# The two kinds of unit in a feed-forward block change places, and five edits go with it

## The chip, the cores and the metric

The kernel runs on one core of one Trainium2 chip. The metric is the device time of one execution in microseconds, as the median of several runs. Five engines of the core work at once, each through a queue of its own in program order: TensorE (PE in the profile; PEld is its weight load), VectorE (DVE), ScalarE (ACT), GpSimd (POOL) and SyncE (SP), which here issues nearly all DMAs. Matrix products are written to PSUM; everything else lies in SBUF.

## The reference

Two layers of an encoder on 512 tokens with 1024 features in float32. Each layer is a half-step feed-forward block, a mixer (attention with twelve heads of 64 in three dilations, and a pooling branch), and a second half-step feed-forward block:

```python
def swiglu(h, w_gate, w_up, w_down):
    return (jax.nn.silu(h @ w_gate) * (h @ w_up)) @ w_down

for l in range(DEPTH):
    x = x + 0.5 * swiglu(rmsnorm(x, ffn1_norm[l]), ffn1_w_gate[l], ffn1_w_up[l], ffn1_w_down[l])
    ...  # mixer: x = x + concat(pooling, attention) @ w_out[l]
    x = x + 0.5 * swiglu(rmsnorm(x, ffn2_norm[l]), ffn2_w_gate[l], ffn2_w_up[l], ffn2_w_down[l])
return rmsnorm(x, final_norm)
```

`rmsnorm` divides by the root of the mean square over the features and multiplies by a gain. The hidden width is 2816.

## The kernel before, in words

x lies transposed in eight tiles of 128 features by 512 tokens, called chunks here. Each float32 operand of a matmul is split into a rounded high part and a low part (the remainder), and a product is three matmuls: high by high, low by high, high by low. For a weight tile ScalarE makes the high part (`whi`, line 357) and VectorE the remainder (`wlo`, line 360).

The hidden width of a feed-forward block is cut into five units of 512 features and one small unit of 256. `UNITS` gives their order; before, the small one (number `NU`) comes first. The gate and up products of a unit are done by Strassen's scheme: seven block products in the order `PORD = (1, 2, 6, 5, 7, 3, 4)` instead of eight. Five of them need sums. On the side of x, `Norm.fold` makes them: for each of the last four chunks ScalarE makes a scaled copy and a high part, and VectorE makes the remainder (`al`, line 446), four sums of 256 columns (`s_n`, lines 447 to 450) and two remainders of these (`sl`, lines 457 and 458). On the side of the weights `total` (lines 254 and 258) makes a pair of sums for product 6, `across` one for product 7 and `every` one for product 4, all on VectorE. Products 1 and 2 need no sums: product 1 works with the first four chunks, product 2 with the last four.

A product of a big unit comes in two steps (cp 0 and 1), each with a weight tile of its own and half of the chunks: 12 matmuls of 512 columns. A product of the small unit is one step with one weight tile: 24 matmuls of 256 columns. `take` gives out weights: it splits two tiles ahead of the one that is taken (`AHEAD`), and makes the sums of a product three places ahead. In each product `px` or `pz` are a pair of PSUM banks; the pools of tags A to D have two banks each. The down matmuls of a unit (`pd_f`, two output chunks per weight tile) stand between the product steps of the next one, at the steps in `DOWN_AT`; each ends in a residual on VectorE (line 708, in the mixer line 937).

The next block's norm works while x is finished: `chunk(c)` folds chunk c and squares it (`square`, on ScalarE), and VectorE adds the squares up (line 480). After the third product (in the mixer, after the first values) `finish_col` sums them over the features with a few matmuls (`ms_n`, line 495), and GpSimd takes the power -0.5.

What runs when on VectorE is decided by three lists: work put into `later` is issued at the next `flush`, `lazy` at the one behind it, `slow` after two. The tables for the rotary embedding are a generator of seven pieces; in the first block a piece is issued after each step from the seventh on in the second unit, and on into the third if some are left.

Of the kernel before, what the change touches and what calls it, by code (L numbers as in the profile page):

```python
# [34 lines left out]
            1.0313385246263351e-05]  # L35
GW = S + 3 * P
NU = 5
UNITS = (NU, 0, 1, 2, 3, 4)
PORD = (1, 2, 6, 5, 7, 3, 4)
DOWN_AT = ((5, 7, 9, 11), (5, 9))  # L40
TWO_PI = 2.0 * math.pi
C1 = 6.28125
C2 = float(np.float32(np.int32(round((TWO_PI - C1) * 2.0**21)) / 2.0**21))
# [35 lines left out]
def trunk(ctx: ExitStack, tc: tile.TileContext, a: dict):  # L79
# [39 lines left out]
    def startup(norm):  # L119
        nc.sync.dma_start(x[0], a["xT"][0])  # L120
        load(2)
        nc.gpsimd.dma_start(vecs, a["vecs"])
        nc.vector.memset(ones, 1.0 / D)
        nc.vector.memset(npow, -0.5)
        idle = const.tile([P, S], mybir.dt.bfloat16, name="idle")
        nc.vector.memset(idle, 0.0)
        nc.scalar.activation(npow, npow, AF.Copy)
        for c in range(1, 4):
            nc.sync.dma_start(x[c], a["xT"][c])
        load()  # L130
        for c in range(4, KD):
            nc.sync.dma_start(x[c], a["xT"][c])
        pump()
        nc.sync.dma_start(ident, a["ident"])
        pos = a["positions"]
        nc.gpsimd.dma_start(col, a["col"])
        nc.gpsimd.dma_start(pos_i, bass.AP(tensor=pos.tensor, offset=pos.offset, ap=[[0, P], [1, S]]))
        warm = bank("D", "warm")
        for _ in range(WARM):
            nc.tensor.matmul(warm, idle[:, 0:P], idle, start=True, stop=True)  # L140
        for c in range(KD):
            norm.fold(c)
            if c < 2:
                divide(c)
            if c == 4:
                divide()
            flush()

# [61 lines left out]
    class Job:  # L210


        def __init__(self, key, n, needs, get, pre=None, done=None):
            self.key, self.n, self.needs, self.get, self.pre, self.done = key, n, needs, get, pre, done
            self.part = None

    jobs, loads = [], []
    AHEAD, SLOTS = 2, 11
    state = {"live": 0, "temps": 0, "load": 0, "split": 0, "taken": 0, "cap": SLOTS}

    def free():
# [7 lines left out]
    def product_jobs(i, l, u):  # L229

        small = u == NU
        cps = 1 if small else 2
        made, out = {}, []

        def quarter(kh, n, cp):
            ap = a[f"gs{i}"][l, kh, n] if small else a[f"gu{i}"][l, u, kh, n, cp]
            made[kh, n, cp] = Load(ap, D)

        quarters = [(0, 0), (1, 0)]
        for kh, n in quarters:  # L240
            for cp in range(cps):
                quarter(kh, n, cp)
        for cp in range(cps):
            quarter(0, 1, cp)
            quarter(1, 1, cp)
        first = next(iter(made.values()))
        first.temps = cps
        loads.extend(made.values())
        both = {}

        def total(cp):

            b11, b12, b22 = (made[q + (cp,)].tile for q in ((0, 0), (0, 1), (1, 1)))
            nc.vector.tensor_tensor(b11, b11, b12, op=ALU.add)
            both[cp] = t4([P, D], F32, f"sum_{i}{l}_{u}_{cp}")
            state["live"] += 1
            state["temps"] -= 1
            nc.vector.tensor_tensor(both[cp], b11, b22, op=ALU.add)

        def across(cp):  # L260
            b12, b22 = made[0, 1, cp].tile, made[1, 1, cp].tile
            nc.vector.tensor_tensor(b12, b12, b22, op=ALU.add)

        def every(cp):
            b21 = made[1, 0, cp].tile
            nc.vector.tensor_tensor(b21, b21, both[cp], op=ALU.add)
            free()

        for p in PORD:
            for cp in range(cps):  # L270
                q = {k: made[k + (cp,)] for k in quarters + [(0, 1), (1, 1)]}
                key = ("g", i, l, u, p, cp)
                tile_of = lambda k, q=q: (lambda: q[k].tile)
                if p == 1:
                    job = Job(key, D, [q[0, 0]], tile_of((0, 0)))
                elif p == 2:
                    job = Job(key, D, [q[1, 0]], tile_of((1, 0)))
                elif p == 6:
                    job = Job(key, D, [q[0, 0], q[0, 1], q[1, 1]], lambda cp=cp: both[cp],
                              pre=lambda cp=cp: total(cp), done=lambda cp=cp: every(cp))  # L280
                elif p == 5:
                    job = Job(key, D, [], tile_of((0, 0)), done=free)
                elif p == 7:
                    job = Job(key, D, [], tile_of((0, 1)), pre=lambda cp=cp: across(cp), done=free)
                elif p == 3:
                    job = Job(key, D, [], tile_of((1, 1)), done=free)
                else:
                    job = Job(key, D, [], tile_of((1, 0)), done=free)
                out.append(job)
        return out  # L290
# [10 lines left out]
    def ffn_jobs(i, l):  # L301
        for n, u in enumerate(UNITS):
            pj = product_jobs(i, l, u)
            dj = down_jobs(i, l, UNITS[n - 1]) if n else []
            for z, job in enumerate(pj):
                jobs.append(job)
                if n and z in DOWN_AT[n == len(UNITS) - 1]:
                    jobs.append(dj.pop(0))
            jobs.extend(dj)
        jobs.extend(down_jobs(i, l, UNITS[-1]))  # L310

# [35 lines left out]
    def divide(half=None):  # L347
# [10 lines left out]

        def rest():
            nc.vector.tensor_tensor(lo[:, o:e], raw[:, o:e], hi[:, o:e].bitcast(F32), op=ALU.subtract)  # L360
            if half != 0 and job.done is not None:
                job.done()
        later.append(rest)
        if half != 0:
            state["split"] += 1
# [1 line left out]
    def take(*key):  # L367
# [2 lines left out]
        state["taken"] += 1  # L370
        while state["split"] < min(i + AHEAD + 1, len(jobs)):
            divide()
        nxt = i + AHEAD + 1
        if nxt < len(jobs) and jobs[nxt].pre is not None and all(ld.tile is not None for ld in jobs[nxt].needs):
            prepare_sums(jobs[nxt])
        pump()
        w, jobs[i].part = jobs[i].part, None
        return w
# [30 lines left out]
    class Norm:  # L409
# [62 lines left out]
        def square(self, c):  # L472
# [111 lines left out]
    def ffn(which, l, norm, nxt, first=False):  # L584
# [20 lines left out]
        def products(n, u):  # L605
            N = S if u < NU else S // 2
            w, cps = N // 2, 2 if u < NU else 1
            xs = [bank("AB"[n % 2], f"px_{nm}_{u}_{i}") for i in range(2)]
            zs = {}
            c = {}  # L610

# [30 lines left out]
            def step(p, cp):  # L642
                flush()
                hi, lo = take("g", which, l, u, p, cp)
                if p == 2 and cp == 0 or p == 5 and cp == 0:
                    zs.clear()
                    zs.update({i: bank("BA"[n % 2], f"pz{p}_{nm}_{u}_{i}") for i in range(2)})
                out = zs if p in (2, 5, 3) else xs
                ks = range(2 * cp, 2 * cp + 2) if cps == 2 else range(4)
                for i in range(2):  # L650
# [22 lines left out]
            for p in PORD:  # L673
                for cp in range(cps):
                    step(p, cp)
                    if turns and z >= 1:
                        for _ in range(2):
                            if turns:
                                turns.pop(0)()
                    if n and z in DOWN_AT[last]:  # L680
                        flush()
                        down(UNITS[n - 1], todo.pop(0))
                    if first and n in (1, 2) and z >= 6:
                        next(rotary, None)
                    z += 1
            tiles = w // P
# [407 lines left out]
```

## Time and profile before

| | |
|---|---|
| runs, us | 1920.46, 1922.04, 1922.73; median 1922.04 |
| profiled execution, us | 1919.58 |
| its span (first to last instruction), us | 1917.8 |
| mean granted clock of TensorE | 0.986 |
| busy, us: TensorE, VectorE, ScalarE, GpSimd | 1857.2 (97%), 1444.4 (75%), 950.4 (50%), 116.9 (6%) |

The profile comes from one execution. Busy time is the time in which an engine had an instruction in work; the granted clock is given as a share of the full 2.4 GHz, so that 0.5 is the lower level of 1.2 GHz. In a timeline each row has the start in us, the duration, the engine, the line of the kernel, the operation, the tile written and those read, the form, and in brackets how long the engine had been idle and what released it. Consecutive VectorE instructions overlap by some 0.08 us, so that the difference of two starts, not the duration, says how long one holds the queue.

The first feed-forward block runs from the start to about 385 us, the first mixer up to 617, the second block of layer 0 up to 969; layer 1 follows in the same way.

### The profile page before, as it was taken

What the parts mean: (1) busy time and instruction counts of PE and PEld (TensorE: products, weight loads), DVE (VectorE), ACT (ScalarE), POOL (GpSimd) and SP (SyncE); (2) the same over time, 40 slices, a digit from 0 to 9 for tenths busy, and PEclk for the clock granted to TensorE, in tenths of its full rate; (3) what the DMA queues carried; (4) which work ended last, traced back from release to release, by engine and by line L of the source; (5) the groups of instructions that cost most, each with busy time, mean ns of one, the idle gap of its engine ahead of it and who ended that gap; (6) DMA issues with size and microseconds to landing.
All of it is one profiled execution on the core that took longest, in us unless ns stands there. A gap on an engine that the chain in (4) does not pass through costs nothing.

```text
span 1917.8 us, 23563 instructions
## 1 busy us (share of the span) xinstructions
PE 1857.2 (97%) x8966; PEld 1551.3 (81%) x8966; DVE 1444.4 (75%) x2041; ACT 950.4 (50%) x1474; POOL 116.9 (6%) x105
## 2 busy tenths in 40 slices
PE   6989999999999999999989999999999989999998
PEld 5868888898877888888878888888888778888887
DVE  6996677647887986778688777675688688777675
ACT  6444344436665553444464444444476565444444
POOL 0000000013230000000000000000323200000000
PEclk7999999999999999999999999999999999999999
DMA  5223333125451233422313322340454223232321
GB/s 183 88 79 100 128 110 107 64 76 145 113 158 56 66 121 99 132 96 97 105 50 116 121 88 88 99 148 17 126 134 126 89 94 116 99 99 96 102 77 45
DMA packets 59696, 194.36 MB, mean 101 GB/s; under 512 B 7920, under 2 KB 8064, under 8 KB 59584
## 3 DMA queue, kind: packets, MB, share of 16 engines
q1 hardware_dynamic: 59440, 192.57, 31.9%
q8 instruction: 70, 1.15, 0.2%
q0 software_dynamic: 144, 0.29, 0.1%
q14 instruction: 42, 0.34, 0.1%
HBM read 171.87 MB, written 2.10 MB: 91 GB/s over the span
## 4 chain that ended last, share of the span: by engine, by line
PE 86%; DVE 8%; ACT 2%; issue 2%; DMA 1%; POOL 1%; SPq 0%; DVEq 0%; POOLq 0%; ACTq 0%
PE pd_f L384 8%; PE pd_f L383 8%; PE pd_f L382 8%; PE px_f L658 8%; PE px_f L655 8%; PE px_f L657 8%; PE pz_f L655 6%; PE pz_f L658 6%; PE pz_f L657 6%; PE pv_m L747 3%; PE ps_m L814 2%; PE pt_m L827 2%; PE pt_f L600 2%; DVE wlo L360 1%; PE po_m L843 1%
## 5 line engine op out<-in xcount | busy, mean ns | idle before, releaser
L360 DVE TENSOR_TENSOR wlo<-raw,whi 128x1024 fp32r<-128x1024 f32 (+2 forms) x421 | 502.0, 1198 | 55.4 <-ACT whi L357 50.4
L357 ACT ACTIVATE whi<-raw 128x1024 fp32r<-128x1024 f32 (+2 forms) x421 | 421.7, 1026 | 220.3 <-DVE wlo L360 63.9
L384 PE MATMUL pd_f<-ah_f,wlo 128*128 128x512 f32 (+1 forms) x736 | 282.2, 383 | 3.1 <-DVE wlo L360 3.1
L382 PE MATMUL pd_f<-ah_f,whi 128*128 128x512 f32 (+1 forms) x736 | 281.5, 382 | 1.0 <-ACT ah_f L400 1.0
L383 PE MATMUL pd_f<-al_f,whi 128*128 128x512 f32 (+1 forms) x736 | 280.7, 381 | 1.0 <-DVE al_f L403 1.0
L708 DVE SCALAR_TENSOR_TENSOR x<-pd_f,x 128x512 f32<-128x512 f32 x184 | 127.0, 690 | 168.8 <-PE pd_f L384 165.5
L592 ACT ACTIVATE c_f<-c_f,rcol_n 128x256 f32<-128x256 f32 (+1 forms) x144 | 70.3, 492 | 272.4 <-DVE c_f L637 102.5
L384 PEld LDWEIGHTS pd_f<-ah_f,wlo 128*128 128x128 f32 x736 | 138.7, 188 | 33.5 <-DVE wlo L360 7.7
L383 PEld LDWEIGHTS pd_f<-al_f,whi 128*128 128x128 f32 x736 | 138.8, 189 | 28.8 <-DVE al_f L403 2.3
L655 PE MATMUL px_f<-whi,ah_n 128*128 128x512 f32 (+1 forms) x384 | 145.9, 380 | 15.7 <-DVE x L937 11.5
L382 PEld LDWEIGHTS pd_f<-ah_f,whi 128*128 128x128 f32 x736 | 138.9, 189 | 27.4 <-ACT ah_f L400 1.9
L655 PE MATMUL px_f<-whi,sh_n 128*128 128x512 f32 (+1 forms) x384 | 144.1, 375 | 5.7 <-ACT c_f L622 5.7
L658 PE MATMUL px_f<-wlo,ah_n 128*128 128x512 f32 (+1 forms) x384 | 145.2, 378 | 1.2 <-DVE wlo L360 1.2
L658 PE MATMUL px_f<-wlo,sh_n 128*128 128x512 f32 (+1 forms) x384 | 144.1, 375 | 1.9 <-DVE wlo L360 1.9
L658 PE MATMUL pz_f<-wlo,sh_n 128*128 128x512 f32 (+1 forms) x384 | 143.3, 373 | 2.1 <-DVE wlo L360 2.1
L657 PE MATMUL px_f<-whi,al_n 128*128 128x512 f32 (+1 forms) x384 | 145.3, 378 | 0.0
L655 PE MATMUL pz_f<-whi,sh_n 128*128 128x512 f32 (+1 forms) x384 | 143.7, 374 | 0.6 <-DVE c_f L624 0.3
L657 PE MATMUL px_f<-whi,sl_n 128*128 128x512 f32 (+1 forms) x384 | 143.7, 374 | 0.0
L657 PE MATMUL pz_f<-whi,sl_n 128*128 128x512 f32 (+1 forms) x384 | 143.1, 373 | 0.0
L819 ACT ACTIVATE e_m<-e_m,nmx_m 128x512 f32<-128x512 f32 x96 | 69.4, 723 | 78.7 <-DVE nmx_m L817 78.1
L655 PEld LDWEIGHTS px_f<-whi,ah_n 128*128 128x128 f32 x384 | 74.3, 193 | 30.1 <-DVE x L937 11.9
L817 DVE CUSTOM_DVE_ANT_0 e_m<-ps_m,gbias 128x512 f32<-128x512 f32 x96 | 65.9, 686 | 33.8 <-PE ps_m L814 33.3
(206 smaller groups left out, 3580.4 us busy)
## 6 DMA issues: line engine op xcount, KB each, us to landing
raw<-in_gu SPq DMA_DIRECT2D x160, 512.0 KB, 3.3
raw<-in_dn SPq DMA_DIRECT2D x80, 512.0 KB, 3.3
raw<-in_wqk SPq DMA_DIRECT2D x24, 512.0 KB, 5.4
qq_m<-hl_q_m SPq DMA_DIRECT2D x48, 256.0 KB, 4.2
raw<-in_wo SPq DMA_DIRECT2D x16, 512.0 KB, 5.3
raw<-in_gs SPq DMA_DIRECT2D x15, 512.0 KB, 4.9
raw<-in_wv SPq DMA_DIRECT2D x16, 384.0 KB, 3.1
kk_m<-hl_k_m SPq DMA_DIRECT2D x48, 128.0 KB, 2.3
```

The source lines that it names most:

```text
L357: nc.scalar.activation(hi[:, o:e], raw[:, o:e], AF.Copy)
L360: nc.vector.tensor_tensor(lo[:, o:e], raw[:, o:e], hi[:, o:e].bitcast(F32), op=ALU.subtract)
L382: nc.tensor.matmul(ps, hi[:, o:o + P], act[0], start=start, stop=False)
L383: nc.tensor.matmul(ps, hi[:, o:o + P], act[1], start=False, stop=False)
L384: nc.tensor.matmul(ps, lo[:, o:o + P], act[0], start=False, stop=stop)
L592: nc.scalar.activation(c[:, :w], src[:, :w], AF.Silu, scale=r)
L655: nc.tensor.matmul(ps, bh, hi[:, o], start=(k == 0 and p in (1, 2, 5)), stop=False, skip_group_check=True)
L657: nc.tensor.matmul(ps, bl, hi[:, o], start=False, stop=False, skip_group_check=True)
L658: nc.tensor.matmul(ps, bh, lo[:, o], start=False, stop=(k == 3), skip_group_check=True)
L708: nc.vector.scalar_tensor_tensor(x[d], ps, 0.5, x[d], op0=ALU.mult, op1=ALU.add)
L817: nc.vector.tensor_tensor_reduce(e, ps, gbias[:, o:o + S], -0.125, 3.0e38, ALU.add, ALU.min, nmx[hd][:, it:it + 1])
L819: nc.scalar.activation(e, e, AF.Exp, bias=nmx[hd][:, it:it + 1], scale=-1.0, accum_out=den[hd][:, it:it + 1])
```

## The change

The unit order becomes one big unit, the small one, then the other four; `DOWN_AT` now has a row for each place in this order. Squares are added on GpSimd. `take` looks at five more jobs instead of one and makes the sums of any whose weights are being loaded and whose sources have been split. A piece of the rotary tables is issued at every fourth step from the third unit on. The PSUM tags A and B of the product banks change places. In the start-up two more weight tiles are loaded between the last pieces of x, and one more is split early. The core of the diff:

```diff
-UNITS = (NU, 0, 1, 2, 3, 4)
+UNITS = (0, NU, 1, 2, 3, 4)
-DOWN_AT = ((5, 7, 9, 11), (5, 9))
+DOWN_AT = ((), (3, 4, 5, 6)) + 3 * ((5, 7, 9, 11),) + ((5, 9),)
...
         for c in range(4, KD):
             nc.sync.dma_start(x[c], a["xT"][c])
+            if c in (5, 7):
+                load()
...
-            if c == 4:
+            if c in (3, 6):
                 divide()
...
-    AHEAD, SLOTS = 2, 11
+    AHEAD, EARLY, SLOTS = 2, 5, 11
...
-        nxt = i + AHEAD + 1
-        if nxt < len(jobs) and jobs[nxt].pre is not None and all(ld.tile is not None for ld in jobs[nxt].needs):
-            prepare_sums(jobs[nxt])
+        for job in jobs[i + AHEAD + 1:i + AHEAD + 1 + EARLY]:
+            if job.pre is not None and job.after.split and all(ld.tile is not None for ld in job.needs):
+                prepare_sums(job)
...
-                lazy.append(lambda: nc.vector.tensor_tensor(acc, acc, sq, op=ALU.add))
+                lazy.append(lambda: nc.gpsimd.tensor_tensor(acc, acc, sq, op=ALU.add))
...
-            xs = [bank("AB"[n % 2], f"px_{nm}_{u}_{i}") for i in range(2)]
+            xs = [bank("BA"[n % 2], f"px_{nm}_{u}_{i}") for i in range(2)]
-                    zs.update({i: bank("BA"[n % 2], f"pz{p}_{nm}_{u}_{i}") for i in range(2)})
+                    zs.update({i: bank("AB"[n % 2], f"pz{p}_{nm}_{u}_{i}") for i in range(2)})
...
-                    if n and z in DOWN_AT[last]:
+                    if z in DOWN_AT[n]:
-                    if first and n in (1, 2) and z >= 6:
+                    if first and n >= 2 and z % 4 == 3:
                         next(rotary, None)
```

How the instructions move is shown at two places. The first is VectorE's queue where layer 0's mixer ends and its second feed-forward block begins, right behind the residual of the last chunk (`x_71`), up to the remainder of the third weight tile. The names are tiles, with a number for each allocation. Before, the rows are:

```order
L480 TENSOR_TENSOR sq_n_0_5140<-sq_n_0_5140,sq_n_6_5291 128x512
L457 TENSOR_TENSOR sl_n_6_5290<-s_n_6_5288,sh_n_6_5289 128x512
L458 TENSOR_TENSOR sl_n_6_5290<-s_n_6_5287,sh_n_6_5289 128x512
L446 TENSOR_TENSOR al_n_3_5175<-xs_n_7_5336,ah_n_3_5174 128x512
L447 TENSOR_TENSOR s_n_7_5339<-xs_n_3_5172,xs_n_7_5336 128x256
L448 TENSOR_TENSOR s_n_7_5340<-s_n_7_5339,xs_n_3_5172 128x256
L449 TENSOR_TENSOR s_n_7_5339<-xs_n_3_5172 128x256
L450 TENSOR_TENSOR s_n_7_5340<-xs_n_7_5336,s_n_7_5340 128x256
L480 TENSOR_TENSOR sq_n_0_5140<-sq_n_0_5140,sq_n_7_5343 128x512
L457 TENSOR_TENSOR sl_n_7_5342<-s_n_7_5340,sh_n_7_5341 128x512
L458 TENSOR_TENSOR sl_n_7_5342<-s_n_7_5339,sh_n_7_5341 128x512
L360 TENSOR_TENSOR wlo_5358<-sum_5_0_5297,whi_5357 128x1024
```

In the changed kernel, right behind the same residual:

```order
L465 TENSOR_TENSOR sl_n_6_5292<-s_n_6_5290,sh_n_6_5291 128x512
L466 TENSOR_TENSOR sl_n_6_5292<-s_n_6_5289,sh_n_6_5291 128x512
L454 TENSOR_TENSOR al_n_3_5175<-xs_n_7_5338,ah_n_3_5174 128x512
L455 TENSOR_TENSOR s_n_7_5341<-xs_n_3_5172,xs_n_7_5338 128x256
L456 TENSOR_TENSOR s_n_7_5342<-s_n_7_5341,xs_n_3_5172 128x256
L457 TENSOR_TENSOR s_n_7_5341<-xs_n_3_5172 128x256
L458 TENSOR_TENSOR s_n_7_5342<-xs_n_7_5338,s_n_7_5342 128x256
L465 TENSOR_TENSOR sl_n_7_5344<-s_n_7_5342,sh_n_7_5343 128x512
L466 TENSOR_TENSOR sl_n_7_5344<-s_n_7_5341,sh_n_7_5343 128x512
L366 TENSOR_TENSOR wlo_5360<-raw_5104,whi_5359 128x1024
L256 TENSOR_TENSOR raw_5102<-raw_5102,raw_5362 128x1024
L260 TENSOR_TENSOR sum_0_1_5385<-raw_5102,raw_5364 128x1024
```

The squares (`sq_n`) are gone from the queue, the third remainder belongs to product 2 of the big unit (`raw_5104`) instead of product 6 of the small one, and the pair of sums for the second half of product 6 (`sum_0_1`) follows it.

The second place is VectorE at the start of layer 1, from the fold of the last chunk on. Before:

```order
L446 TENSOR_TENSOR al_n_3_8007<-xs_n_7_8135,ah_n_3_8006 128x512
L447 TENSOR_TENSOR s_n_7_8138<-xs_n_3_8004,xs_n_7_8135 128x256
L448 TENSOR_TENSOR s_n_7_8139<-s_n_7_8138,xs_n_3_8004 128x256
L449 TENSOR_TENSOR s_n_7_8138<-xs_n_3_8004 128x256
L450 TENSOR_TENSOR s_n_7_8139<-xs_n_7_8135,s_n_7_8139 128x256
L457 TENSOR_TENSOR sl_n_6_8111<-s_n_6_8109,sh_n_6_8110 128x512
L458 TENSOR_TENSOR sl_n_6_8111<-s_n_6_8108,sh_n_6_8110 128x512
L480 TENSOR_TENSOR sq_n_0_7936<-sq_n_0_7936,sq_n_7_8142 128x512
L457 TENSOR_TENSOR sl_n_7_8141<-s_n_7_8139,sh_n_7_8140 128x512
L458 TENSOR_TENSOR sl_n_7_8141<-s_n_7_8138,sh_n_7_8140 128x512
L360 TENSOR_TENSOR wlo_8160<-sum_5_0_8083,whi_8159 128x1024
L266 TENSOR_TENSOR raw_7730<-raw_7730,sum_5_0_8083 128x1024
```

In the changed kernel:

```order
L454 TENSOR_TENSOR al_n_3_8009<-xs_n_7_8135,ah_n_3_8008 128x512
L455 TENSOR_TENSOR s_n_7_8138<-xs_n_3_8006,xs_n_7_8135 128x256
L456 TENSOR_TENSOR s_n_7_8139<-s_n_7_8138,xs_n_3_8006 128x256
L457 TENSOR_TENSOR s_n_7_8138<-xs_n_3_8006 128x256
L458 TENSOR_TENSOR s_n_7_8139<-xs_n_7_8135,s_n_7_8139 128x256
L465 TENSOR_TENSOR sl_n_6_8111<-s_n_6_8109,sh_n_6_8110 128x512
L466 TENSOR_TENSOR sl_n_6_8111<-s_n_6_8108,sh_n_6_8110 128x512
L256 TENSOR_TENSOR raw_7746<-raw_7746,raw_7916 128x1024
L260 TENSOR_TENSOR sum_0_1_8163<-raw_7746,raw_7966 128x1024
L465 TENSOR_TENSOR sl_n_7_8141<-s_n_7_8139,sh_n_7_8140 128x512
L466 TENSOR_TENSOR sl_n_7_8141<-s_n_7_8138,sh_n_7_8140 128x512
L366 TENSOR_TENSOR wlo_8160<-raw_7768,whi_8159 128x1024
```

Here the second pair of sums (`sum_0_1`) stands ahead of the third remainder.

## Rows read from the trace of the kernel before

**Rows 1.** windows by stretch: span us, then busy us (instructions) by engine, clock, DMA

```profile
7.00:55.00 48.00, 33.37 (x176) 30.13 (x177) 38.24 (x66) 31.30 (x54) 1.03 (x1) 0.72 0.45 164
92.00:135.00 43.00, 36.37 (x153) 27.78 (x153) 42.05 (x59) 20.00 (x30) 0.00 (x0) 0.96 0.27 86
135.00:360.00 225.00, 225.00 (x1021) 186.34 (x1020) 162.63 (x188) 98.80 (x131) 0.00 (x0) 1.00 0.34 111
617.00:647.00 30.00, 23.73 (x177) 23.02 (x176) 26.05 (x43) 17.22 (x30) 1.02 (x1) 0.89 0.25 82
968.00:999.00 31.00, 22.97 (x164) 21.56 (x163) 27.53 (x46) 16.55 (x29) 1.01 (x1) 0.89 0.25 77
```

**Rows 2.** timeline of PE behind the first mixer: start, us, what [idle before]

```profile
616.88 0.39 PE L384 MATMUL po_m<-yhh_m,wlo 128*128 128x512 f32 x1
617.11 0.28 PE L655 MATMUL px_f<-whi,ah_n 128*128 128x256 f32 x1
617.22 0.28 PE L657 MATMUL px_f<-whi,al_n 128*128 128x256 f32 x1
...
624.47 0.58 PE L655 MATMUL px_f<-whi,ah_n 128*128 128x256 f32 x1 [5.76 <-DVE x L937]
...
634.53 0.95 PE L495 MATMUL ms_n<-ones,sq_n 128*128 128x1 f32 x8
```

**Rows 3.** timeline of PE in the stretch of the rotary tables

```profile
103.73 0.63 PE L382 MATMUL pd_f<-ah_f,whi 128*128 128x512 f32 x1
104.16 0.63 PE L383 MATMUL pd_f<-al_f,whi 128*128 128x512 f32 x1
```

**Rows 4.** timeline of DVE behind the first mixer

```profile
620.52 0.69 DVE L446 TENSOR_TENSOR al_n<-xs_n,ah_n 128x512 fp32r<-128x512 f32 x1
621.13 0.42 DVE L447 TENSOR_TENSOR s_n<-xs_n,xs_n 128x256 f32<-128x256 f32 x1
...
622.59 1.22 DVE L360 TENSOR_TENSOR wlo<-raw,whi 128x1024 fp32r<-128x1024 f32 x1
623.73 0.68 DVE L937 TENSOR_TENSOR x<-po_m,x 128x512 f32<-128x512 f32 x1
624.33 0.68 DVE L480 TENSOR_TENSOR sq_n<-sq_n,sq_n 128x512 f32<-128x512 f32 x1
...
630.51 1.23 DVE L360 TENSOR_TENSOR wlo<-sum,whi 128x1024 fp32r<-128x1024 f32 x1 [0.18 <-ACT whi L357]
```

**Rows 5.** groups by line and form: busy us, mean ns | idle before

```profile
L480 DVE TENSOR_TENSOR sq_n<-sq_n,sq_n 128x512 f32<-128x512 f32 x42 | 28.8, 685 | 0.6
```

**Rows 6.** timeline of DVE at the end of the attention, layer 0

```profile
557.21 1.70 DVE L403 TENSOR_TENSOR yh_m<-y_m,yh_m 128x512 fp32r<-128x512 f32 x1
558.83 2.32 DVE L360 TENSOR_TENSOR wlo<-raw,whi 128x1024 fp32r<-128x1024 f32 x1
561.07 0.68 DVE L403 TENSOR_TENSOR pl_m<-pt_m,ph_m 128x512 fp32r<-128x512 f32 x1
```

**Rows 7.** timeline of POOL in the same stretch

```profile
558.43 1.64 POOL L908 TENSOR_TENSOR m_pool_m<-r_pool_m,ic_pool_m 64x512 f32<-64x512 f32 x1
560.14 2.14 POOL L909 TENSOR_TENSOR m_pool_m<-m_pool_m,v_pool_m 128x512 f32<-128x512 f32 x1
```

**Rows 8.** timeline of DVE at the start of layer 1

```profile
963.60 0.69 DVE L708 SCALAR_TENSOR_TENSOR x<-pd_f,x 128x512 f32<-128x512 f32 x1 [0.29 <-PE pd_f L384]
...
984.43 1.22 DVE L360 TENSOR_TENSOR wlo<-sum,whi 128x1024 fp32r<-128x1024 f32 x1
```

**Rows 9.** timeline of PE at the start of layer 1

```profile
968.84 0.28 PE L655 MATMUL px_f<-whi,ah_n 128*128 128x256 f32 x1
...
988.43 0.95 PE L495 MATMUL ms_n<-ones,sq_n 128*128 128x1 f32 x8
```

**Rows 10.** timeline of DVE in the start-up

```profile
14.03 0.69 DVE L446 TENSOR_TENSOR al_n<-xs_n,ah_n 128x512 fp32r<-128x512 f32 x1 [0.94 <-ACT ah_n L439]
```

**Rows 11.** timeline of PE in the start-up

```profile
41.00 1.28 PE L495 MATMUL ms_n<-ones,sq_n 128*128 128x1 f32 x8 [2.55 <-DVE sq_n L480]
```

More of the change, by code (lines that the diff above doesn't have):

```diff
@@ L214, in __init__ @@
             self.key, self.n, self.needs, self.get, self.pre, self.done = key, n, needs, get, pre, done
-            self.part = None
+            self.part, self.after, self.split = None, None, False
     jobs, loads = [], []
-    AHEAD, SLOTS = 2, 11
+    AHEAD, EARLY, SLOTS = 2, 5, 11
     state = {"live": 0, "temps": 0, "load": 0, "split": 0, "taken": 0, "cap": SLOTS}
@@ L232, in product_jobs @@
         cps = 1 if small else 2
-        made, out = {}, []
+        made, out, firsts = {}, [], {}
         def quarter(kh, n, cp):
@@ L275, in product_jobs @@
                     job = Job(key, D, [q[0, 0]], tile_of((0, 0)))
+                    firsts[cp] = job
                 elif p == 2:
@@ L280, in product_jobs @@
                               pre=lambda cp=cp: total(cp), done=lambda cp=cp: every(cp))
+                    job.after = firsts[cp]
+                    firsts[cp] = job
                 elif p == 5:
@@ L284, in product_jobs @@
                     job = Job(key, D, [], tile_of((0, 1)), pre=lambda cp=cp: across(cp), done=free)
+                    job.after = firsts[cp]
                 elif p == 3:
@@ L306, in ffn_jobs @@
                 jobs.append(job)
-                if n and z in DOWN_AT[n == len(UNITS) - 1]:
+                if z in DOWN_AT[n]:
                     jobs.append(dj.pop(0))
@@ L360, in rest @@
             nc.vector.tensor_tensor(lo[:, o:e], raw[:, o:e], hi[:, o:e].bitcast(F32), op=ALU.subtract)
-            if half != 0 and job.done is not None:
-                job.done()
+            if half != 0:
+                job.split = True
+                if job.done is not None:
+                    job.done()
         later.append(rest)
@@ L679, in products @@
                                 turns.pop(0)()
-                    if n and z in DOWN_AT[last]:
+                    if z in DOWN_AT[n]:
                         flush()
                         down(UNITS[n - 1], todo.pop(0))
-                    if first and n in (1, 2) and z >= 6:
+                    if first and n >= 2 and z % 4 == 3:
                         next(rotary, None)
```

## The prediction

> **What bounds the kernel now.** I read the table of engines first: TensorE is busy nearly throughout, so nothing can be won but its idle time and its slow time. The windows by stretch, read next, say where these are. In the long middle of the first feed-forward block TensorE is busy for all of 225 us at full clock while VectorE is busy for 162.6 of them [rows 1]: there the change can win nothing. Time is lost in the start-up, in the stretch of the rotary tables (6.6 of 43 us idle, mean clock 0.96), and at the other block starts, at 617 and 968 us (6.3 and 8.0 us idle, mean clock 0.89 [rows 1]; a third, behind the second mixer, is like the first). There VectorE is busy for 26.05 of 30 and 27.53 of 31 us, and TensorE waits for it. So VectorE's queue at the block starts sets the time, and I walk it through.
>
> The paces come from the timeline. At full clock a 512-column matmul follows the last one after some 0.227 us (0.23 in the row) and a 256-column one after 0.12 [rows 2]; at half clock the former takes 0.43 [rows 3]. A product step of the small unit is 24 matmuls of 256 columns, 2.88 us; a step of a big unit is 12 of 512 columns, 2.72 us, and a product takes two steps. On VectorE, start to start, a weight remainder (wlo) takes 1.14 us, a pair of weight sums of the same size, the second waiting for the first, 2.4, a fold remainder (al, sl) 0.60, the four fold sums 1.46, a residual or a square 0.60 [rows 4].
>
> **The change part by part.** *Tables.* Seven pieces of table work stood in eight successive steps of one unit; now they stand three steps apart or more, over three units. In their place TensorE waited for remainders behind the pieces. Going away: 6.6 us idle [rows 1] and 1.5 us of half pace (seven matmuls around 104 us, 0.2 each [rows 3]). What is late next: in its unit VectorE has the first three pieces to carry, sixteen operations of at most a square's 0.60 us, under 10 us, and little slack, so I put 0.6 back. Sum -7.5.
>
> *Squares on GpSimd.* 42 additions of 0.685 us leave VectorE [rows 5]. The trace of before shows no GpSimd work beside the folds, but it shows some beside remainders. A weight remainder that takes 1.22 us [rows 4] takes 2.32 when it starts under a GpSimd instruction: that one ends at 560.07, the remainder 1.08 later. The remainder in front took 1.70 instead of 0.68, and GpSimd's next instruction, begun under the long one, goes on for 1.1 us after its end [rows 6, 7]. Each side waits for the other to finish, and every time they meet VectorE loses 1.0 to 1.1 us. Its operations there have two operands in SBUF, as weight remainders, weight sums, fold sums and fold remainders all have; one with an operand in PSUM (pl_m) ran beside GpSimd in 0.68 [rows 6]. So a moved square saves VectorE 0.60 and costs it 1.1 where its queue is full. The bounds are -0.60 (it falls beside a PSUM operation or a wait) and +0.5 for each; I take +0.5, as the nearest row, except where the walk shows a gap. The Trainium skill, "SBUF — State Buffer", section "SBUF: two separate sides", says that the shared pair of ports is an exclusive lock, that the one that starts first has it for its whole instruction, and that the other is blocked; the 2.32 against 1.22 us agrees. By that rule alone short VectorE operations in a row could keep GpSimd out; in the rows GpSimd gets in at the next boundary.
>
> *Block starts behind a mixer (two of them).* Before, the third remainder, for the summed weights, starts at 630.51 and is done 1.14 later, at 631.65 [rows 4]; the third product step follows at once and the matmuls on the squares at 634.53. That is 17.42 us since 617.11 for three steps worth 8.64: 8.8 lost. Part of it is the wait of 5.76 us for the residual that frees a PSUM bank [rows 2]; the new tags take this wait away. What is late next is the remainders. In the new queue the second big step's remainder stands before the last residual, as before, and the third behind the last fold. In front of it are the same residuals, folds, one sum pair and remainders as before 631.65, less seven squares (-4.2) plus seven blocks by GpSimd (7.7), of which some 0.8 fall on short waits for ScalarE: 2.7 later, 634.35. TensorE by then has done two steps and two matmuls more, 5.9 us since 617.11: 11.3 lost. Behind it the second sum pair and a remainder (3.5 us) hold the fourth step for up to 1.3 us, or half pace after the idle time costs 2.0. From the fourth step on TensorE has enough remainders. So 12.7 lost instead of 8.8: +3.9 each, +7.8 in all. With the adds for nothing, the same walk gives 6.85: -2.0 each.
>
> *Block start of the second layer.* Here VectorE waits for TensorE until the sixth residual at 963.60, so three adds fall in gaps. The third remainder of before starts at 984.43 [rows 8] and is done at 985.57, 21.97 behind that residual; three steps are done at 988.43, 10.9 us lost since 968.84 [rows 9]. Now both sum pairs stand ahead of the third remainder (+2.4), four squares are gone (-2.4), four adds come (+4.4, of which 0.6 beside a residual): 989.4. TensorE has done 5.9 us of work by then: 14.7 lost, and 2.0 of half pace, since it has stood for 10 us: +5.8. With the adds for nothing +1.5: the sums five blocks ahead are what makes it late.
>
> *Start-up.* Before, the first three products are done at 41.0 [rows 11]: 32.4 lost, and 1.3 of half pace behind it, 33.7. In the new queue VectorE starts its unbroken run some 0.4 us earlier than at 14.03 [rows 10], since the second half of the first product takes a whole tile. Up to the sixth step's remainder it holds 5 remainders (5.7), 4 al (2.4), 4 times the fold sums (5.9), 8 sl (4.8), two sum pairs (4.8) and two updates of weights (2.3): 25.9, and seven adds (7.7): 47.3. Six steps (16.3 us of work) end at 50.2: 33.9 lost, +0.2. With the adds for nothing they end at 44.8: -5.2. The weight tiles that now stand between the last pieces of x delay these; ScalarE comes to them late, behind its own queue, which hides it.
>
> *The rest.* The same product and down matmuls run in another order; in the middle of a block VectorE has 62 us to spare in 225 [rows 1], which hides the moved downs and the small unit. The last unit and the end are as before.
>
> Sum: -7.5 + 7.8 + 5.8 + 0.2 = +6.3. The profiled execution took 1919.58 us, 1.78 over its span, and gives 1925.9; the median of the runs is 1922.04, 2.46 above it, so the forecast for it is 1928.3.
>
> **The rivals.** *First: the adds hide.* If GpSimd's additions fall beside residuals, copies and waits, the squares are a pure gain for VectorE: -7.5, -2.0 twice, +1.5, -5.2, together -15.2: 1906.8. For it: VectorE waits for ScalarE now and then in the folds, and residuals read PSUM. Against it: 26.05 of 30 us busy [rows 1], and both meetings in the rows cost a full microsecond [rows 6]. The Trainium skill, "Perfetto Trace Analysis", section "Optimizing Scalar/DVE Operations", says that with VectorE saturated it may make sense to give work to GpSimd, and warns in the same place that the two share a read port, so that it might not help; by the first half alone it would be this rival's time, and the rows bear out the second half. *Second: half of them hide.* Every VectorE instruction between two adds is short, and an add that comes during a residual costs half. Then the four starts come to half-way between both sums: -4.4, 1917.6, the smallest of gains. *Third: a new wait behind unit 0.* The small unit's second step writes the PSUM pair that the Silu and the multiply of unit 0's last product read. Only one step of 2.88 us lies between, where before a big unit left two, 5.45. On VectorE two remainders and a sum pair (4.7 us) stand ahead of that multiply. If it is 1 to 2 us late in each of the four blocks, 4 to 8 us are added: 1932 to 1936. It decides if ScalarE's Silu is late too; in the steady part VectorE has slack, so I hold it for unlikely.
>
> **How the numbers follow.** Forecast 0.50 (1922 to 1935 by the unsure half pace, +-1 per mixer start, and +-3 at the start-up), first rival 0.20, second 0.18 (1913 to 1922), third 0.12. What this kernel's measurement can tell from no change is about 0.2%, 3.8 us: faster means below 1918.2, slower above 1925.9. Faster is the first rival and over half of the second: 0.30. Within: the rest of the second and the lower edge of the forecast, 0.18. Slower 0.52. The range 1907 to 1937 takes in the first rival's time, as its chance is too large to leave out.
>
> **What would show it.** Right, if the stretch of the tables has no wait of TensorE above 0.5 us; if at the two mixer starts TensorE no longer waits for the residual but for the second and third remainders, about 5.8 and 3.6 us; if in the second layer's start it stands about 10 us before the third step; and if fold sums or remainders of VectorE take a microsecond more beside each of GpSimd's adds, which themselves stretch where the two meet. Wrong, if the adds stand beside residuals and the folds keep their 0.42 and 0.69 us [rows 4]: then the third remainders come 6 us earlier than in my walk and the time is the first rival's. Wrong too, if waits come up in the middle of the blocks.

## The result, and the profile after

| | before | changed |
|---|---|---|
| median of runs, us | 1922.12 | 1940.57 (1939.95 to 1940.75) |
| profiled execution, us (span) | 1919.58 (1917.8) | 1939.95 (1938.0) |
| mean granted clock | 0.986 | 0.980 |

The ratio is 1.0097 (95% interval 1.0079 to 1.0114): the change makes the kernel 18.4 us slower. The forecast was 6.3 us slower, 1928.3 us, with a range of 1907 to 1937.

To find the place I add up, for each stretch, what TensorE loses: the time from one matmul's start to the next less the steady pace at full clock (0.227 us for 512 columns and 0.120 for 256, as in the prediction; 0.173 for 384, the median of the trace). Waits and half pace, that is matmuls at the lower clock, both count. In us:

| stretch | before | changed | difference | forecast |
|---|---|---|---|---|
| start-up (to 92 us before, to 130 after) | 28.1 | 29.5 | +0.5, since the first matmul comes 0.9 earlier | +0.2 |
| tables and the rest of the first block | 11.0 | 15.2 | +4.2 | -7.5 |
| start behind mixer 0 | 9.1 | 14.0 | +4.9 | +3.9 |
| start of layer 1 | 11.3 | 16.3 | +5.0 | +5.8 |
| start behind mixer 1 | 9.1 | 14.5 | +5.4 | +3.9 |
| all else: what the spans leave | | | +0.2 | 0.0 |

The five stretches add up to 20.0; the two spans differ by 20.2, the medians by less, since the profiled execution of before was a short one. One line is wrong, by 11.7 of the 13.7 us between this sum and the forecast's 6.3. The windows of the changed kernel (columns as in [rows 1]) show it first: the 35 us with the fourth table piece, a steady part, then the starts behind mixer 0 and of layer 1.

```profile
165.00:200.00 35.00, 28.34 (x123) 22.26 (x122) 32.91 (x42) 15.46 (x22) 0.00 (x0) 0.95 0.14 47
270.00:385.00 115.00, 114.53 (x520) 94.39 (x519) 77.55 (x94) 50.97 (x70) 3.94 (x3) 1.00 0.30 99
621.00:651.00 30.00, 22.05 (x73) 16.04 (x73) 28.60 (x35) 15.71 (x22) 2.91 (x2) 0.77 0.13 41
978.00:1009.00 31.00, 19.32 (x69) 14.55 (x68) 30.76 (x42) 15.69 (x23) 2.68 (x2) 0.78 0.11 36
```

At 165 us TensorE stands for 6.7 of 35 us while VectorE is busy for 32.9. At the two starts VectorE has almost no idle time left (28.60 of 30, before 26.05; 30.76 of 31, before 27.53), and the clock is 0.77 and 0.78 where it was 0.89 [rows 1].

*The tables.* TensorE's timeline has its longest waits behind the first, the fourth and the seventh piece, all of them a remainder that is late; the second row of the middle group shows the half pace (0.42 us to the next start) that follows:

```profile
137.89 0.50 PE L392 MATMUL pd_f<-ah_f,wlo 128*128 128x512 f32 x1 [1.63 <-DVE wlo L366]
...
196.52 0.79 PE L392 MATMUL pd_f<-ah_f,wlo 128*128 128x512 f32 x1 [5.00 <-DVE wlo L366]
197.12 0.63 PE L390 MATMUL pd_f<-ah_f,whi 128*128 128x512 f32 x1
197.54 0.63 PE L391 MATMUL pd_f<-al_f,whi 128*128 128x512 f32 x1
...
261.77 0.50 PE L392 MATMUL pd_f<-ah_f,wlo 128*128 128x512 f32 x1 [1.41 <-DVE wlo L366]
```

VectorE in front of the wait of 5.00 us (a row with x2 or x3 holds so many instructions in a row):

```profile
188.49 1.28 DVE L632 TENSOR_TENSOR c_f<-pz_f,c_f 128x512 f32<-128x512 f32 x2
189.69 1.41 DVE L161 SCALAR_TENSOR_TENSOR turn<-far,turn 128x512 f32<-128x512 f32 x2
191.13 0.43 DVE L157 TENSOR_SCALAR kmul<-turn 128x512 f32<-128x512 f32 x1
191.59 0.43 DVE L158 TENSOR_SCALAR kmul<-kmul 128x512 f32<-128x512 f32 x1
192.06 2.14 DVE L161 SCALAR_TENSOR_TENSOR turn<-kmul,turn 128x512 f32<-128x512 f32 x3
194.12 1.22 DVE L264 TENSOR_TENSOR raw<-raw,raw 128x1024 f32<-128x1024 f32 x1
195.25 1.22 DVE L366 TENSOR_TENSOR wlo<-raw,whi 128x1024 fp32r<-128x1024 f32 x1
```

The piece holds the queue from 189.69 to 194.12, 4.4 us, and a sum for product 7 (line 264, made early by the new rule) another 1.1; the remainder behind them is what TensorE waits for. Why nothing hides the piece is in three windows of before, in a unit without tables: the second to the sixth product step, the down matmuls behind the sixth, and the later steps.

```profile
303.00:319.00 16.00, 16.00 (x81) 13.39 (x80) 15.58 (x17) 7.88 (x13) 0.00 (x0) 1.00 0.24 81
319.00:324.00 5.00, 5.00 (x23) 3.98 (x22) 5.00 (x7) 2.60 (x4) 0.00 (x0) 1.00 0.48 163
324.00:352.00 28.00, 28.00 (x125) 23.17 (x125) 18.85 (x23) 12.92 (x17) 0.00 (x0) 1.00 0.54 179
```

VectorE is busy for 15.58 of the first 16 us (sums, remainders, activations), for all of the next 5, and for 18.85 of the later 28. Nearly all its slack here lies in the later steps, from the seventh on, and a piece behind the fourth step falls into the full part.

*The start behind mixer 0* answers to [rows 2, 4]. TensorE of the changed kernel:

```profile
625.71 0.50 PE L663 MATMUL px_f<-whi,ah_n 128*128 128x512 f32 x1 [0.99 <-ACT whi L363]
...
630.71 0.80 PE L666 MATMUL px_f<-wlo,ah_n 128*128 128x512 f32 x1 [4.26 <-DVE wlo L366]
...
638.00 0.79 PE L663 MATMUL pz_f<-whi,ah_n 128*128 128x512 f32 x1 [2.66 <-ACT whi L363]
```

The wait for the residual is gone, and waits for the second and third step's weights stand in its place, as forecast. Of what TensorE loses here, waits are 7.9 us (6.1 before) and half pace 5.9 (2.9 before): more of the growth is clock than wait. The third is put down to ScalarE's high part, whose queue shows that it too was held by VectorE's folds:

```profile
635.86 0.63 ACT L461 ACTIVATE sh_n<-s_n 128x512 fp32r<-128x512 f32 x1 [2.66 <-DVE s_n L458]
636.39 0.61 ACT L462 ACTIVATE sh_n<-s_n 128x512 fp32r<-128x512 f32 x1
636.91 1.99 ACT L363 ACTIVATE whi<-raw 128x1024 fp32r<-128x1024 f32 x2
```

GpSimd's last three adds of this start, and the VectorE instructions that run into them:

```profile
618.47 1.55 POOL L488 TENSOR_TENSOR sq_n<-sq_n,sq_n 128x512 f32<-128x512 f32 x1 [4.78 <-ACT sq_n L482]
624.86 1.37 POOL L488 TENSOR_TENSOR sq_n<-sq_n,sq_n 128x512 f32<-128x512 f32 x1 [4.84 <-ACT sq_n L482]
633.34 1.53 POOL L488 TENSOR_TENSOR sq_n<-sq_n,sq_n 128x512 f32<-128x512 f32 x1 [7.11 <-ACT sq_n L482]
```

```profile
618.90 1.40 DVE L456 TENSOR_TENSOR s_n<-s_n,xs_n 128x256 f32<-128x256 f32 x1
...
625.01 1.77 DVE L465 TENSOR_TENSOR sl_n<-s_n,sh_n 128x512 fp32r<-128x512 f32 x1
...
633.84 1.31 DVE L456 TENSOR_TENSOR s_n<-s_n,xs_n 128x256 f32<-128x256 f32 x1
```

A fold sum takes 1.40 and 1.31 us instead of 0.42 [rows 4], a fold remainder 1.77 instead of 0.68: each meeting costs 0.9 to 1.1 us. The Trainium skill's rule in "SBUF — State Buffer", section "SBUF: two separate sides" (one side holds the shared ports for its whole instruction), agrees.

*The start of layer 1* answers to [rows 9]:

```profile
978.30 0.39 PE L663 MATMUL px_f<-whi,ah_n 128*128 128x512 f32 x1
...
984.97 0.80 PE L666 MATMUL px_f<-wlo,ah_n 128*128 128x512 f32 x1 [3.34 <-DVE wlo L366]
...
994.74 0.79 PE L663 MATMUL pz_f<-whi,ah_n 128*128 128x512 f32 x1 [5.80 <-ACT whi L363]
...
998.50 0.79 PE L666 MATMUL pz_f<-wlo,ah_n 128*128 128x512 f32 x1 [2.54 <-DVE wlo L366]
```

TensorE stands for 3.34 and 5.80 us ahead of the third step's first matmul, and 2.54 more for that step's remainder.

*The start-up.* GpSimd's last four adds, VectorE's first two remainders beside them, and TensorE:

```profile
37.57 8.31 POOL L488 TENSOR_TENSOR sq_n<-sq_n,sq_n 128x512 f32<-128x512 f32 x4 [0.62 <-ACT sq_n L482]
```

```profile
38.02 2.29 DVE L366 TENSOR_TENSOR wlo<-raw,whi 128x1024 fp32r<-128x1024 f32 x1
40.23 2.29 DVE L366 TENSOR_TENSOR wlo<-sum,whi 128x1024 fp32r<-128x1024 f32 x1
```

```profile
40.37 0.79 PE L666 MATMUL pz_f<-wlo,ah_n 128*128 128x512 f32 x1 [9.64 <-DVE wlo L366]
...
50.84 0.16 PE L503 MATMUL ms_n<-ones,sq_n 128*128 128x1 f32 x1
```

Each remainder takes 2.29 us instead of 1.22 [rows 4], and six steps are done at 50.84 (forecast 50.2).

### The profile page after: what moved, and what is told of

The parts are those of the page before. It is cut to its first block, busy times and chain, and to the rows that moved or that the text cites. A ratio compares the mean times of both kernels' runs of the same rounds, so it can differ in the third digit from the quotient of the medians.

```text
span 1938.0 us, 23628 instructions
## 1 busy us (share of the span) xinstructions
PE 1861.2 (96%) x8966; PEld 1548.1 (80%) x8966; DVE 1441.4 (74%) x1999; ACT 954.9 (49%) x1474; POOL 178.2 (9%) x147
## 4 chain that ended last, share of the span: by engine, by line
PE 86%; DVE 9%; issue 2%; ACT 2%; DMA 1%; SPq 0%; POOL 0%; DVEq 0%; POOLq 0%; ACTq 0%
PE pd_f L392 8%; PE pd_f L391 8%; PE pd_f L390 8%; PE px_f L666 7%; PE px_f L663 7%; PE px_f L665 7%; PE pz_f L663 6%; PE pz_f L666 6%; PE pz_f L665 6%; PE pv_m L755 3%; DVE wlo L366 2%; PE ps_m L822 2%; PE pt_m L835 2%; PE pt_f L608 2%; PE po_m L851 1%
## 5 line engine op out<-in xcount | busy, mean ns | idle before, releaser
L392 PEld LDWEIGHTS pd_f<-ah_f,wlo 128*128 128x128 f32 x736 | 138.8, 189 | 39.4 <-DVE wlo L366 13.5
L488 POOL TENSOR_TENSOR sq_n<-sq_n,sq_n 128x512 f32<-128x512 f32 x42 | 61.1, 1454 | 1120.5 <-ACT sq_n L482 1120.1
L666 PEld LDWEIGHTS px_f<-wlo,ah_n 128*128 128x128 f32 x384 | 74.0, 193 | 29.3 <-DVE wlo L366 16.7
```

The source lines that it names most:

```text
L392: nc.tensor.matmul(ps, lo[:, o:o + P], act[0], start=False, stop=stop)
L488: lazy.append(lambda: nc.gpsimd.tensor_tensor(acc, acc, sq, op=ALU.add))
L666: nc.tensor.matmul(ps, bh, lo[:, o], start=False, stop=(k == 3), skip_group_check=True)
```

## The experiments

After the result the theory was: a table piece at the fourth step costs its own length, the adds cost what the prediction said. The main rival: the sums made five blocks ahead fill VectorE's queue, there and at the starts. The runs below were made in three groups, each beside runs of the kernel before on the same chip. A name with b is the kernel before with an edit, one with e the changed kernel with an edit. The ratio is to the runs of before in the same group, with its 95% interval; differences between kernels are taken from the ratios, on 1922 us, and those of the changed kernel to an e are known to some 4 us. The last five columns are us lost by TensorE in one profiled execution, as in the table above.

| kernel | median, us | ratio | start-up | tables | mixer 0 | layer 1 | mixer 1 |
|---|---|---|---|---|---|---|---|
| before (first profile) | 1922.1 | 1 | 28.1 | 11.0 | 9.1 | 11.3 | 9.1 |
| changed | 1940.6 | 1.0097 (1.0079-1.0114) | 29.5 | 15.2 | 14.0 | 16.3 | 14.5 |
| b1 | 1924.0 | 1.0004 (0.9995-1.0013) | 27.2 | 12.8 | 9.1 | 14.6 | 9.1 |
| e1 | 1927.2 | 1.0026 (1.0017-1.0036) | 28.5 | 4.4 | 13.5 | 17.3 | 15.0 |
| e2 | 1929.9 | 1.0036 (1.0023-1.0048) | 29.2 | 13.2 | 13.3 | 13.6 | 13.3 |
| e3 | 1932.2 | 1.0046 (1.0033-1.0058) | 27.4 | 15.1 | 10.7 | 15.6 | 11.3 |
| e5 | 1910.6 | 0.9935 (0.9922-0.9947) | 28.6 | 3.2 | 10.1 | 12.3 | 10.1 |
| b2 | 1932.7 | 1.0049 (1.0035-1.0062) | 32.2 | 11.0 | 10.9 | 12.3 | 10.9 |
| b3 | 1912.9 | 0.9949 (0.9936-0.9961) | 28.1 | 3.5 | 9.1 | 12.8 | 9.1 |
| b5 | 1915.2 | 0.9955 (0.9942-0.9967) | 29.0 | 3.4 | 9.1 | 13.3 | 10.3 |
| e6 | 1937.1 | 1.0077 (1.0063-1.0091) | 28.7 | 3.1 | 17.2 | 18.2 | 17.9 |
| e4 | 1920.1 | 0.9986 (0.9978-0.9995) | 28.4 | 3.2 | 13.2 | 13.6 | 13.2 |

**b1, the tables' edit alone, in the kernel before.**

```diff
-                    if first and n in (1, 2) and z >= 6:
+                    if first and n >= 2 and z % 4 == 3:
```

> The kernel before with one edit: a table piece at every fourth step from the third unit on, as in the changed kernel. Theory (place): at the fourth step of a unit VectorE has no slack, since the sums and remainders of product 6 pass there, so a piece costs TensorE about its own length, whatever the unit order and the sums' rule. The stretch of the tables then loses about as much as in the changed kernel (9.7 us of waits instead of 6.65): 1923 to 1927 us, a single wait of TensorE of 4 to 5 us behind the longest piece. Rival (sums): the front of a unit is full only because the changed kernel makes the sums five blocks ahead; with the old rule the pieces at the fourth step cost half or less: waits of under 4 us in the stretch, 1917 to 1920 us. The prediction had 7.5 us less for this edit: 1914.5 us.

Between the two, at the lower edge of the theory (1922.9 us on the first before): 0.8 us slower, not told apart from no change. The wait behind the longest piece is there in the old order and with the old rule for the sums:

```profile
192.22 0.50 PE L384 MATMUL pd_f<-ah_f,wlo 128*128 128x512 f32 x1 [4.23 <-DVE wlo L360]
```

The three pieces behind a fourth step make waits of 2.33, 4.23 and 1.29 us. The stretch loses 12.8 us; before 11.0. So the edit by itself gives back nothing of what it takes away, and 2.4 of the 15.2 in the changed kernel come from elsewhere.

**e1, the pieces in other places, in the changed kernel.**

```diff
-                    if first and n >= 2 and z % 4 == 3:
+                    if first and n >= 2 and z in (7, 9):
```

> The changed kernel with the table pieces issued behind the 8th and the 10th step of a unit instead of every fourth. Theory (place): there VectorE has 1 to 2 us to spare in each step and the sums are done, so the waits of 1.6, 1.7, 5.0 and 1.4 us between 137 and 262 us go but for 1 or 2 us, and with the half pace behind them 10 to 12.5 us: 1928 to 1931 us. Rival (sums): the sums made early make VectorE late at the start of each unit by themselves, at least half of the waits stay: 1934 to 1937 us.

13.6 us less than the changed kernel by the ratios (0.0071 of 1922), 10.8 of them in the tables' stretch (15.2 to 4.4): a little more than the theory. The window that answers to 165:200 above:

```profile
165.00:200.00 35.00, 34.43 (x159) 28.04 (x158) 28.91 (x32) 18.17 (x26) 0.00 (x0) 1.00 0.24 84
```

TensorE's idle time falls from 6.66 to 0.57 us and the clock stays at 1.00. It is the place that costs.

**e2, the sums one job ahead, as by the old rule** (the new test that the sources have been split stays).

```diff
-    AHEAD, EARLY, SLOTS = 2, 5, 11
+    AHEAD, EARLY, SLOTS = 2, 1, 11
```

> The changed kernel with EARLY = 1, that is with the sums of weights made only one job beyond the split ones, as before. Theory (place): the wait of 5.0 us behind the fourth piece stays above 4 us; only the start of layer 1 gains, where the second pair of sums no longer stands ahead of the third remainder (2.4 us by the prediction's walk): 1937 to 1939 us. Rival (sums): the two sums for product 7 (2.3 us) leave the front of the unit, the wait at 196.5 us falls below 3 us, those at 171 to 179 us go: with the start of layer 1 1931 to 1935 us.

11.7 us less, better than either expected. TensorE's wait behind the fourth piece stays above 4 us, as the theory had it; at the start of layer 1 the last wait, for the remainder, is gone:

```profile
194.27 0.79 PE L392 MATMUL pd_f<-ah_f,wlo 128*128 128x512 f32 x1 [4.24 <-DVE wlo L366]
...
979.02 0.50 PE L666 MATMUL px_f<-wlo,ah_n 128*128 128x512 f32 x1 [0.95 <-DVE wlo L366]
...
989.07 0.79 PE L663 MATMUL pz_f<-whi,ah_n 128*128 128x512 f32 x1 [7.47 <-ACT whi L363]
```

The profiled execution, the longest of e2's five, is 8.5 us shorter than that of the changed kernel: 2.7 at layer 1, 2.0 in the tables, 0.7 and 1.2 behind the mixers, 1.9 elsewhere. So the early sums cost a little at several places, and 3 us of the 11.7 are not placed. The theory had the wait in the tables right and its sum too small.

**e3, the squares back on VectorE.**

```diff
-                lazy.append(lambda: nc.gpsimd.tensor_tensor(acc, acc, sq, op=ALU.add))
+                lazy.append(lambda: nc.vector.tensor_tensor(acc, acc, sq, op=ALU.add))
```

> The changed kernel with the squares added on VectorE again. By the prediction's walk an add on GpSimd costs VectorE 1.1 us against 0.60 for its own, so this gains 0.5 for each in the full queues: 3.5 us at the start-up, 2.7 at each of the two starts behind a mixer, 2.0 at layer 1: together 10.9, 1929.7 us. Rival (the adds hide): GpSimd's adds stand beside other work, each costs VectorE under 0.3 us, and taking them back makes the kernel slower by 8 to 15 us: 1949 to 1956 us. Between them, if a block costs as much as an add: 1938 to 1943 us.

9.8 us less (expected 10.9): 2.1 at the start-up (3.5), 3.3 and 3.2 behind the mixers (2.7), 0.7 at layer 1 (2.0). The prediction's net price of the squares holds in size; the rival is refuted.

**e5, the changed kernel without those three edits** (the diffs of e1, e2 and e3 together).

> The changed kernel with three edits out at once: table pieces behind the 8th and 10th step, EARLY = 1, squares on VectorE. What is left of the change is the unit order, the PSUM tags, the places of the down products and the loads at the start. If the three costs found one by one (13.6, 11.7 and 9.8 us against the changed kernel by ratio) were independent, the time would be 1905 us; but the sums cost part of their price through the tables (2.0 us of waits there), and some of the rest is spread, so theory: the stretches add up to 27 us lost at the start, 3 in the tables, 10 to 11 at each start behind a mixer, 12.5 at layer 1: 1909 to 1914 us. Rival: the order itself costs at the block starts (the big unit's remainders come faster than VectorE makes them), each of the three starts stays above 12.5 us lost: 1916 to 1921 us.

Right: 12.5 us faster than before, the fastest of all. Singly the three edits cost 13.6 + 11.7 + 9.8 = 35.1 us, together 31.1 (0.0162 of 1922), so they add up within what the runs can tell.

**b2, the squares on GpSimd, in the kernel before** (e3's diff turned round).

> The kernel before with one edit: squares added on GpSimd. Theory (each add blocks VectorE for 1.1 us where its queue is full): dearer by 2 to 4 us at the start-up, 3 at each start behind a mixer, 1 to 2 at layer 1: 1931 to 1934 us, and VectorE's instructions beside an add 1.0 to 1.1 us longer. Rival (it is the new unit order that puts the adds beside the remainders; in the old order they fall in waits): within 2 us of before: 1920 to 1924 us.

9.4 us slower: the price of an add does not come from the new order. Behind mixer 0 the same VectorE instructions grow as in the changed kernel (a fold sum 1.40 us, a fold remainder 1.76). A part is another wait, since here the sum of the squares is wanted at the third product, and GpSimd has it late (before, this wait was 2.55 [rows 11]); and the residual that frees the PSUM bank comes later too (5.76 [rows 2]):

```profile
44.37 0.37 PE L495 MATMUL ms_n<-ones,sq_n 128*128 128x1 f32 x1 [6.98 <-POOL sq_n L480]
...
630.51 0.58 PE L655 MATMUL px_f<-whi,ah_n 128*128 128x256 f32 x1 [6.79 <-DVE x L937]
```

**b3, the pieces behind the 8th and 10th step, in the kernel before.**

```diff
-                    if first and n in (1, 2) and z >= 6:
+                    if first and n >= 1 and z in (7, 9):
```

> The kernel before with one edit: table pieces behind the 8th and the 10th step of a unit, from the second unit on. Theory (place): the waits of 6.6 us and 1.5 to 2 us of half pace between 92 and 135 us go but for about 1 us: 1914.5 to 1917 us. Rival: pieces delay remainders wherever they stand, half of it stays: 1918 to 1920 us.

9.8 us faster, more than the theory: the stretch goes from 11.0 to 3.5, just the 7.5 of the prediction's term, and the other four differ by at most 1.5. So the term was there to be had; the change put the pieces where it could not be.

**b5, the PSUM tags on top of b3.**

```diff
-            xs = [bank("AB"[n % 2], f"px_{nm}_{u}_{i}") for i in range(2)]
+            xs = [bank("BA"[n % 2], f"px_{nm}_{u}_{i}") for i in range(2)]
...
-                    zs.update({i: bank("BA"[n % 2], f"pz{p}_{nm}_{u}_{i}") for i in range(2)})
+                    zs.update({i: bank("AB"[n % 2], f"pz{p}_{nm}_{u}_{i}") for i in range(2)})
```

> The kernel before with two edits: table pieces behind the 8th and 10th step, and the PSUM tags A and B of the product banks changed. The tags take away the wait of 5.76 us for the residual at the two starts behind a mixer. Theory: VectorE's queue sets the third remainder there (631.65 us), so TensorE waits for it instead, and at most 1 us is gained at each: 1912 to 1917 us. Rival: the residual's wait is what costs, without it 3 us and more are gained at each: 1907 to 1910 us.

No different from b3 (0.9955 and 0.9949). The wait for the residual is gone, and the start behind mixer 0 loses 9.1 us as before, since the remainder of the next product is waited for instead:

```profile
616.50 0.58 PE L658 MATMUL pz_f<-wlo,ah_n 128*128 128x256 f32 x1 [3.48 <-DVE wlo L360]
```

**e6, e5 with the squares added later on VectorE**, from the fourth step on instead of between the folds.

```diff
-                lazy.append(lambda: nc.vector.tensor_tensor(acc, acc, sq, op=ALU.add))
+                (lazy if self.n % 3 == 1 else self.adds).append(lambda: nc.vector.tensor_tensor(acc, acc, sq, op=ALU.add))
...
+                if not n and p in (2, 6) and norm.adds and (p, cp) != (2, 0):
+                    later.extend(norm.adds[:3])
+                    del norm.adds[:3]
```

> The version without the three costs (old table places replaced by the 8th and 10th step, sums one ahead, squares on VectorE), with one more edit: VectorE adds the squares up behind the fourth and fifth step of the block instead of between the folds, since their sum is wanted only behind the sixth step. Theory (each add in front of the third product's operands costs 0.60 us): three to five adds leave the queue there, 1 to 3 us less at each of the three later starts and at the start-up: 1903 to 1908 us. Rival (VectorE is busy without a gap until the sixth step, so the adds only delay a later remainder): 1909 to 1912 us, with new waits of TensorE behind the fifth and sixth step.

A miss for both: 1937.1 us, 27 us more than e5 by the ratios, of which the three later starts show 20.8. VectorE has the sum late at the sixth step, and TensorE, whose queue holds the matmuls on the squares in front of the rest, stands for 6.88 us:

```profile
640.08 0.34 PE L505 MATMUL ms_n<-ones,sq_n 128*128 128x1 f32 x1 [6.88 <-DVE sq_n L488]
```

**e4, e5 with the squares on GpSimd.**

> The changed kernel with tables behind the 8th and 10th step and EARLY = 1, the squares left on GpSimd. It differs from the version without the three costs (1910.6 us) in the squares alone. Theory (an add blocks VectorE for 1.1 us wherever both meet): 8 to 10 us dearer than that: 1918.5 to 1921 us. Rival (the price of the squares found in the changed kernel was that of a queue made too full by the early sums): under 4 us: 1911 to 1914.5 us.

Right: 9.8 us by the ratios (0.0051 of 1922), the same as in e3's fuller queue. By stretch it is 3.1 behind each mixer, 1.3 at layer 1 and nothing at the start-up (28.4 and 28.6). The adds do hold VectorE up at the start-up too: a remainder beside them takes 2.33 us at 40.23 us, and TensorE's longest wait for one is 5.10 us, against 3.08 in e5. Other waits are shorter there, so that the sums come out alike; why stays open.

In these two executions the price behind a mixer is largely clock. The windows behind mixer 0, first e4, then e5:

```profile
609.00:639.00 30.00, 24.22 (x86) 17.95 (x85) 28.18 (x35) 16.80 (x23) 3.06 (x2) 0.77 0.17 58
608.00:638.00 30.00, 24.28 (x102) 18.82 (x101) 27.77 (x38) 16.79 (x24) 1.02 (x1) 0.94 0.24 84
```

TensorE is idle equally long (5.8 and 5.7 us), with waits of 0.95, 2.08 and 2.72 us in e4 and of 1.03, 4.10 and 0.53 in e5, but the granted clock is 0.77 in the one and 0.94 in the other: half pace takes 6.4 and 3.1 us. Behind mixer 1 waits make 1.2 of the difference and half pace 1.9. It is not so everywhere: what e3 gains behind mixer 1 is waits alone.

## Why the prediction was wrong

- *Tables: -7.5 forecast, +4.2 measured; this is the step that failed.* "... in its unit VectorE has the first three pieces to carry, sixteen operations of at most a square's 0.60 us, under 10 us, and little slack, so I put 0.6 back." It asked how far apart the pieces stand and not behind which step, put 0.6 us on them without a walk of the queue, and knew VectorE's spare time only as a sum, 62 us in 225. Nearly all of it lies behind the sixth step. Three pieces were put behind a fourth step, where 15.58 of 16 us are taken, and each became a wait (1.63, 5.00, 1.41 us, with half pace behind the longest); the prediction's sign was no wait above 0.5. b1 shows it without the other edits, e1 and b3 give the 7.5 and more back by the place alone. The early sums add 2.0 in this stretch (e2), a cost that the prediction counted at layer 1 only.
- *Squares: the price right, the count wrong.* Meetings cost 0.9 to 1.1 us (1.0 to 1.1 said), moving all the adds 9.8 us (e3, e4; the walk gives 10.9). But the walk let all seven adds of a mixer start meet a full queue. The first three (607 to 612 us) fall beside residuals and waits, and no VectorE instruction there is more than 0.21 us longer, so that four meetings cost 3.9 us where the walk had 6.9. It also counted 4.2 us saved for seven squares; where the first three were taken out, VectorE's waits grew from 0.9 to 2.5 us. The sum came out partly by luck.
- *Starts behind a mixer: right but small*, +4.9 and +5.4 for +3.9. The third step could begin at 638.00, 16.3 us behind the first matmul, and its remainder was there 1.1 later, 17.4 (forecast 17.24). The waits were 4.26 and 2.66 us (5.8 and 3.6 said). Half pace was put at up to 2.0, a figure that no row gives; it was 5.9. That the new tags give nothing because the remainder is late next is shown by b5.
- *Layer 1: right in sum*, +5.0 for +5.8. TensorE stood for 9.1 us before the third step (10 said), 2.5 more for its remainder, and half pace was 4.4 (2.0 said). The early sums were given 2.4 there; e2 gives 2.7.
- *Start-up: right*, +0.5 for +0.2.
- *Rivals.* Hidden adds, whole or by half, are refuted by e3, e4 and b2. The first rival's time was summed wrongly besides: 6.85 behind a mixer and 44.8 at the start-up do not follow from the walk, which without its 6.9 and 7.7 us for the adds gives some 5.8 and 42.5 and so a time below 1906.8. No wait for a PSUM bank stands behind unit 0: the third rival did not come up.

What stays open: e5's 2.7 us on b3 (0.0014, intervals that overlap) may be the order, the tags or the loads at the start, which were not tried apart. By stretch e5 loses 1.0 more than b3 behind each mixer and 0.5 less at layer 1, and its first matmul comes 1.2 us earlier (6.38 and 7.61 us).

## What to carry to other kernels

Before work is spread over a queue, read the queue's slack by step, not by block: here a piece of 4.4 us cost TensorE a wait of 5.00 us behind the fourth step and no piece behind the eighth or tenth more than 0.57. An add moved from VectorE to GpSimd saved 0.6 us and cost about 1 where VectorE worked on two SBUF operands without a break; beside PSUM reads and waits it cost 0.2 at most, but no run here had a gain from it. And work that is issued earlier (sums, here) takes its time from what stood in that place.

## What the runs showed of the hardware

The same code with the same wait can go on at either level of the clock. In front of the second step of layer 1 TensorE waits for 2.91 us in before and in b1, with the same instructions around it. TensorE in before:

```profile
975.02 0.39 PE L658 MATMUL pz_f<-wlo,ah_n 128*128 128x256 f32 x1 [2.91 <-DVE wlo L360]
975.25 0.28 PE L655 MATMUL pz_f<-whi,ah_n 128*128 128x256 f32 x1
975.36 0.28 PE L657 MATMUL pz_f<-whi,al_n 128*128 128x256 f32 x1
```

And in b1:

```profile
974.89 0.58 PE L658 MATMUL pz_f<-wlo,ah_n 128*128 128x256 f32 x1 [2.91 <-DVE wlo L360]
975.27 0.42 PE L655 MATMUL pz_f<-whi,ah_n 128*128 128x256 f32 x1
975.49 0.42 PE L657 MATMUL pz_f<-whi,al_n 128*128 128x256 f32 x1
```

In before the matmuls of 256 columns behind the wait go on 0.11 us apart, the full level; in b1 0.22 apart, the lower level. The 42 us from 968 on have a granted clock of 0.92 in the one and 0.76 in the other. This start loses 11.3 us in the one and 14.6 in the other, and so single executions of one kernel may differ by 3 us from this alone. The runs of before went from 1919.0 us with a mean clock of 0.988 to 1926.5 with 0.980. What decides between the two levels is not shown.
